# The output stage of a hybrid encoder layer in written order on every engine, with the sums of the first column group made in DRAM

## The chip, the core and the metric

The kernel runs on one core of a Trainium2 chip. Five engines work side by side: TensorE (PE, with its weight loads PEld), VectorE (DVE), ScalarE (ACT), GpSimd (POOL) and SyncE (SP, which only issues transfers). Each works through its own instructions in order; semaphores tie them together. Transfers run on 16 DMA engines and are issued from SP's queue or POOL's. The metric is the device time of one execution in microseconds (us).

## The reference

One layer over 512 tokens of width 2048, in float32. A combined projection `w_in` gives queries, keys, values, the attention's gate and the two inputs of a linear recurrent unit (LRU). Attention (8 heads) and the LRU (both directions) each give 1024 columns; each is normed as a group, and one output projection mixes both:

```python
h = rms_norm(x, norm_w)
proj = jnp.einsum('bsd,de->bse', h, w_in)
q, k, v, g_attn, xr, g_lru = jnp.split(proj, SPLITS, axis=-1)
attn_out = attention_group(q, k, v, q_norm_w, k_norm_w)
lru_out = lru_group(xr, conv_w, conv_b, lru_wa, lru_ba, lru_wx, lru_bx, lru_lambda)
mixed = jnp.concatenate([rms_norm(attn_out, attn_norm_w) * jax.nn.silu(g_attn),
                         rms_norm(lru_out, lru_norm_w) * jax.nn.silu(g_lru)], axis=-1)
return x + jnp.einsum('bse,ed->bsd', mixed, w_out)
```

The last line, `mixed` times `w_out` (512x2048 by 2048x2048) plus x, is the output stage.

## The kernel before

**Arithmetic.** A float32 operand is split into a rounded part `h` and a rest `l`; a product is three matmuls, hh + hl + lh. ScalarE makes `h` by a cast (`wh`), VectorE makes `l` by a subtraction (`wl`). A matmul is 128x128 by 128x512, written "mm" or "pj" after the PSUM bank it sums into.

**Stages.** The start transposes x, sums its squares and runs the first projection (0 to 57 us), with `rstd` per token on POOL (`rsqrt_mean`, L264 and L265), spread to the row `rbc` by `rows` (L275, L276, L278, a matmul L284 and a copy L285); then `evac_bc` (L383) multiplies projection results by `rbc`. The LRU's halves and the projections of keys, values and queries follow, woven with each other (to 279 us); the attention, woven with gate projections (279 to 446); the last two gate projections with the norms of both groups (446 to 507.5; the row scales of the attention's norm are `group_rstd`, L664 and L668, and `rows` again, `gbc`); and the output stage (507.6 to 682).

**The output stage.** 512x2048 by 2048x2048 is done in blocks of 2 by 2 by 2: seven products of blocks instead of eight. Its eight row pairs `i` (256 rows of `w_out` each) are gone through for two column groups `g` of 1024 columns. For each group a first half runs the pairs with products P1, Q6, Q5, Q7 (24 matmuls a pair), a second half with Q3, P2, Q4 (18 a pair). I number the pairs of halves 0 to 31: 0 to 7 and 8 to 15 are the halves of group 0, 16 to 23 and 24 to 31 those of group 1. Left sides (`mh`, `ml`) are built before, by `build`. The right sides are two blocks of `w_out` or sums of them: T1 and T3 are two-block sums (`t1`, `t30`, `t31`), T2 is x's first part plus a block, T4 is T2 plus another block. A right side for two products is a tile of 2 x 512 columns, `x_` or `y_`, which `split` (L720 cast, L721 subtraction) makes into `wh` and `wl`, in one of four buffers by turns, so a pair takes two of them.

Before the change, T1 and T3 are summed in DRAM: a copy on SP's queue and an accumulating transfer on POOL's (`sums_of_blocks`, L741 to L744, one row pair at each eighth fill step of the second projection; T1's accumulation in `other_sums`, L750, at the end of the query projection). T2 is `y_[:, 0] + x_[:, 0]` on VectorE (L790), is written to DRAM (`t2`, L792, POOL's queue) and read back in the second half (L833), where VectorE adds the other block (L836).

**What sets the order.** Except at the start, where more engines are written by hand, only TensorE's order is the written one. On the other engines a scheduler orders instructions, with the output stage's loads, splits and sums put early by a priority:

```python
SOON = 150
with tc.high_priority(SOON):
    nc.sync.dma_start(y_[:, 0], block(m, 1, 2 * g))
    nc.sync.dma_start(y_[:, 1], t3[g][m])
    xb = split(x_)
    nc.vector.tensor_add(y_[:, 0], y_[:, 0], x_[:, 0])
    yb = split(y_)
    nc.gpsimd.dma_start(t2[m], y_[:, 0])
```

Tiles loaded there come from two rings (`wring`, three tiles; `aring`, four) and a few kept buffers, so a load waits until the tile's former content has been split. In the attention POOL scales each weight tile (`weights`, L591), once per iteration; the tile is turned and used two iterations later.

Of the kernel before, what the change touches and what calls it, by code (L numbers as in the profile page):

```python
# [16 lines left out]
P = 128  # L17
# [41 lines left out]
def hybrid_kernel(  # L59
# [133 lines left out]
    loads_done, powers = {}, []  # L193
# [68 lines left out]
    def rsqrt_mean(dst, src, n, width):  # L262

        nc.gpsimd.tensor_scalar(dst, src, 1.0 / n, EPS, op0=ALU.mult, op1=ALU.add)  # L264
        powers[:] = [nc.gpsimd.tensor_tensor(dst, dst, nhalf[:, :width], op=ALU.pow).ins]  # L265
# [312 lines left out]

    def weights(q, g, t):
# [11 lines left out]
        nc.gpsimd.tensor_scalar(p, p, sm, 0.0, op0=ALU.mult, op1=ALU.add)  # L591
# [30 lines left out]
    def attention(rots):  # L622
# [4 lines left out]
        for i in range(last + 3):  # L627
            h, t = divmod(i, NT)
            if i < last:
                ps_[i] = weights(qs[h], h // G, t)  # L630
                if t == 0 and h + 2 < NH:
                    qs[h + 2] = turned(rots[(h + 2) // G], (h + 2) % G)
# [78 lines left out]
    def split(blocks):  # L711
# [7 lines left out]
        hi, lo = (t[:, : blocks.shape[1]] for t in (hi, lo))  # L719
        nc.scalar.copy(hi, blocks)  # L720
        nc.vector.tensor_sub(lo, blocks, f(hi))  # L721
# [5 lines left out]
    t1, t2, t30, t31 = (  # L727
        dram.tile([NP, P, SEQ + 16], F32, name=t, tag=t)[:, :, :SEQ] for t in ("t1", "t2", "t30", "t31")
# [7 lines left out]
    def sums_of_blocks():  # L736

        for m in range(NP):
            with tc.issue_after(loads_done[nc.sync]):
                for g in range(2):  # L740
                    nc.sync.dma_start(t3[g][m], block(m, 0, 2 * g))  # L741
                nc.sync.dma_start(t1[m], block(m, 0, 0))
            for g in range(2):
                nc.gpsimd.dma_start(t3[g][m], block(m, 1, 2 * g), accum_op=ALU.add)  # L744
            yield

    def other_sums():
        with tc.issue_after(*powers):
            for m in range(NP):
                nc.gpsimd.dma_start(t1[m], block(m, 0, 1), accum_op=ALU.add)  # L750

    def outputs(g, places, work):
# [3 lines left out]


        xs = [
            pools["out"].tile([P, NT, SEQ], F32, tag=t, bufs=1, name=nm(t)) for t in ("xt", "cb")
        ]  # L760

        def banks(*kinds):
            return [[kind() for _ in range(2)] for kind in kinds]

        def product(k, dst, i, b, n):
# [9 lines left out]
        p1, q6, q5, q7 = banks(*((mm, mm, pj, pj), (pj, mm, mm, pj))[g])  # L775
        for i in range(8):
            m = mixed[i][0] // (2 * P)
            with tc.high_priority(SOON):

                x_, y_ = next(places)(), next(places)()  # L780
                if g == 0:
                    nc.sync.dma_start(x_[:, 0], t1[m])
                    nc.sync.dma_start(x_[:, 1], block(m, 0, 1))
                else:
                    nc.sync.dma_start(x_.rearrange("p j e -> p (j e)"), block(m, 0, 2 * g, 2))
                    nc.vector.tensor_add(x_[:, 0], x_[:, 0], x_[:, 1])
                nc.sync.dma_start(y_[:, 0], block(m, 1, 2 * g))
                nc.sync.dma_start(y_[:, 1], t3[g][m])
                xb = split(x_)
                nc.vector.tensor_add(y_[:, 0], y_[:, 0], x_[:, 0])  # L790
                yb = split(y_)
                nc.gpsimd.dma_start(t2[m], y_[:, 0])  # L792
            next(work, None)
            for k, dst, b, n in ((P1, p1, xb, 1), (Q6, q6, yb, 0), (Q5, q5, xb, 0), (Q7, q7, yb, 1)):
                product(k, dst, i, b, n)
        with tc.high_priority(SOON):

            for s in range(2):
                nc.scalar.copy(xs[1][:, 2 + s], p1[s])
            for s in range(2):  # L800
                nc.vector.tensor_sub(xs[1][:, s], xs[1][:, 2 + s], q6[s])  # L801
            for s in range(2):
                nc.vector.tensor_sub(xs[0][:, 2 + s], q5[s], xs[1][:, s])  # L803
            for s in range(2):
                nc.vector.tensor_add(xs[0][:, s], q7[s], xs[0][:, 2 + s])  # L805
                nc.vector.tensor_sub(xs[1][:, s], xs[1][:, s], q7[s])  # L806

        def leave(t, j, queue, e0=0, e1=SEQ):
            c0 = (2 * g + j) * SEQ
            queue.dma_start(of[tokens[t], c0 + e0 : c0 + e1], xs[j][:, t, e0:e1])  # L810

        def residual(m, j):

            with tc.high_priority(SOON):
                xr = pools["fin"].tile([P, 2, SEQ], F32, tag="t4", bufs=2, name=nm("t4"))
# [5 lines left out]
            to = xs[j][:, 2 * m : 2 * m + 2]  # L821
            nc.vector.tensor_add(to, to, xr)  # L822

        q3, p2, q4 = banks(*((mm, mm, pj), (pj, mm, mm))[g])

        def second(i):
            m = mixed[i][0] // (2 * P)
            ring = (wring, aring)[i % 2]
# [15 lines left out]
        for i in range(8 - 2 * g):  # L844
            for step in second(i):
                step()
            if 1 <= i < 5:
                residual((i - 1) // 2, (i - 1) % 2)
# [267 lines left out]
```

## Time and profile before

| | |
|---|---|
| median of 3 runs (lowest, highest) | 689.21 us (688.12, 689.9) |
| the profiled execution, its time / its span | 688.86 us / 687.1 us |
| busy, share of the span: PE, DVE, ACT, POOL | 96%, 70%, 50%, 14% |
| mean granted TensorE clock | 0.981 |
| matmuls of the output stage (L771) | 672 |
| first L771 matmul, last L771 matmul | 507.58 us, 682.02 us |
| HBM read, written | 91.42 MB, 20.97 MB |

In a row of the timeline the columns are start, duration (us), engine, line, operation, out<-in, shapes, and in brackets the idle time before it with what ended it. "SPq" rows are transfers that SP issues. A DMA engine share is a mean over 16. In a row of groups, "busy, mean ns of one" and then the idle time before them with its releasers. A matmul's duration includes its drain, so start to start tells the pace.

### The profile page before, as it was taken

How to read it: one execution, taken by the hardware profiler on the slowest of the kernel's cores; microseconds unless marked ns; L12 is line 12 of the kernel's file. 1: busy time of each engine (PE TensorE's matmuls, PEld its weight loads, DVE VectorE, ACT ScalarE, POOL GpSimd, SP SyncE). 2: the span in 40 equal slices, each digit the busy share in tenths (PEclk: the TensorE clock that was granted, in tenths of full speed). 3: DMA queues.
4: the chain of work that ended last, by engine and by line, in shares of the span. 5: the costliest groups of instructions: out<-in, count | busy, mean ns of one | idle time of the engine just before them, and what ended most of it. 6: DMA issues, size and time to landing. Idle time of an engine off the chain costs nothing. (4 is left out here: it accounts for less than half of the span.)

```text
span 687.1 us, 8648 instructions
## 1 busy us (share of the span) xinstructions
PE 660.7 (96%) x3059; PEld 543.8 (79%) x3059; DVE 482.7 (70%) x788; ACT 340.2 (50%) x590; POOL 97.1 (14%) x137
## 2 busy tenths in 40 slices
PE   9998999999999999999999999979989989889997
PEld 6886888888888888888888888858868867668775
DVE  5868789968688747557655675788268677766774
ACT  3523798589668316445543474534245433234430
POOL 0011100100033105311222221000001102210010
PEclk9999999999999999999999999989989999999999
DMA  8867786842233323921122122214375848896562
GB/s 278 276 179 206 174 205 174 232 98 89 92 125 122 92 62 69 207 62 59 34 62 62 62 62 62 62 61 124 92 236 180 303 138 268 262 288 216 176 199 93
DMA packets 54140, 100.38 MB, mean 146 GB/s; under 512 B 4568, under 2 KB 14928, under 8 KB 54096
## 3 DMA queue, kind: packets, MB, share of 16 engines
q1 hardware_dynamic: 47088, 81.99, 37.8%
q0 software_dynamic: 6688, 17.31, 10.8%
q10 hardware_dynamic: 320, 0.53, 0.3%
q8 instruction: 24, 0.39, 0.2%
q14 instruction: 20, 0.16, 0.1%
HBM read 91.42 MB, written 20.97 MB: 164 GB/s over the span
## 5 line engine op out<-in xcount | busy, mean ns | idle before, releaser
L148 PE MATMUL pj<-x,wh 128*128 128x512 f32 x376 | 150.4, 400 | 2.8 <-DVE ev L383 2.8
L150 PE MATMUL pj<-x,wl 128*128 128x512 f32 x376 | 147.9, 393 | 0.0
L149 PE MATMUL pj<-x,wh 128*128 128x512 f32 x376 | 147.5, 392 | 0.0
L212 ACT CAST wh<-wr 128x512 fp32r<-128x512 f32 x143 | 85.9, 618 | 72.4 <-PE pj L150 25.9
L213 DVE TENSOR_TENSOR wl<-wr,wh 128x512 fp32r<-128x512 f32 x144 | 101.1, 725 | 29.0 <-ACT wh L212 24.9
L720 ACT CAST wh<-wr 128x1024 fp32r<-128x1024 f32 x64 | 60.0, 944 | 99.3 <-PE mm L771 61.3
L148 PEld LDWEIGHTS pj<-x,wh 128*128 128x128 f32 x376 | 71.4, 190 | 16.8 <-issue 3.2
L150 PEld LDWEIGHTS pj<-x,wl 128*128 128x128 f32 x376 | 71.1, 189 | 15.5
L149 PEld LDWEIGHTS pj<-x,wh 128*128 128x128 f32 x376 | 71.4, 190 | 14.0 <-DVE x L241 0.3
L148 PE MATMUL pj<-wh,x 128*128 128x512 f32 x192 | 74.9, 390 | 0.0
L150 PE MATMUL pj<-wh,x 128*128 128x512 f32 x192 | 74.7, 389 | 0.0
L149 PE MATMUL pj<-wl,x 128*128 128x512 f32 x192 | 74.7, 389 | 0.0
L721 DVE TENSOR_TENSOR wl<-wr,wh 128x1024 fp32r<-128x1024 f32 x64 | 67.2, 1085 | 9.3 <-ACT wh L720 9.1
L771 PE MATMUL mm<-wl,mh 128*128 128x512 f32 x128 | 51.9, 406 | 5.9 <-DVE wl L721 5.8
L771 PE MATMUL mm<-wh,mh 128*128 128x512 f32 x128 | 51.2, 400 | 1.9 <-ACT wh L720 1.9
L771 PE MATMUL mm<-wh,ml 128*128 128x512 f32 x128 | 51.2, 400 | 0.0
L600 ACT CAST b<-mm 128x512 fp32r<-128x512 f32 x32 | 18.8, 586 | 62.2 <-PE mm L598 62.2
L586 DVE TENSOR_REDUCE mx<-mm 128x1 f32<-128x512 f32 x32 | 22.1, 690 | 33.2 <-PE mm L150 32.4
L771 PE MATMUL pj<-wl,mh 128*128 128x512 f32 x96 | 39.0, 407 | 4.8 <-DVE wl L721 4.8
L150 PEld LDWEIGHTS pj<-wh,x 128*128 128x128 f32 x192 | 36.0, 188 | 7.6
L148 PEld LDWEIGHTS pj<-wh,x 128*128 128x128 f32 x192 | 36.0, 188 | 7.4
L149 PEld LDWEIGHTS pj<-wl,x 128*128 128x128 f32 x192 | 36.0, 188 | 7.4
(207 smaller groups left out, 1123.7 us busy)
## 6 DMA issues: line engine op xcount, KB each, us to landing
wr<-in_w_in_dram SPq DMA_DIRECT2D x71, 512.0 KB, 3.6
wr<-in_w_out_dram SPq DMA_DIRECT2D x24, 512.0 KB, 5.3
wr<-t SPq DMA_DIRECT2D x40, 256.0 KB, 5.1
t<-in_w_out_dram SPq DMA_DIRECT2D x24, 256.0 KB, 5.2
t<-in_w_out_dram POOLq DMA_DIRECT2D x24, 256.0 KB, 6.2
wr<-in_w_out_dram SPq DMA_DIRECT2D x24, 256.0 KB, 4.4
t<-wr POOLq DMA_DIRECT2D x16, 256.0 KB, 4.1
t<-in_x_dram POOLq DMA_DIRECT2D x8, 512.0 KB, 6.1
```

The source lines that it names most:

```text
L148: nc.tensor.matmul(acc, lh, rh, start=start, stop=False)
L149: nc.tensor.matmul(acc, lh, rl, start=False, stop=False)
L150: nc.tensor.matmul(acc, ll, rh, start=False, stop=stop)
L212: copy(hi, raw[:, k, :])
L213: nc.vector.tensor_sub(lo, raw[:, k, :], f(hi))
L586: nc.vector.tensor_reduce(mx, sc, axis=AX.X, op=ALU.max, negate=True)
L600: nc.scalar.copy(pth[:, :, tt], p3)
L720: nc.scalar.copy(hi, blocks)
L721: nc.vector.tensor_sub(lo, blocks, f(hi))
L771: nc.tensor.matmul(dst[s], lh[:, ts_], rh, start=i == 0 and j == 0, stop=i == 7 and j == 2)
```

## The change

It has four parts.

1. The output stage of all engines (ACT, DVE, SP, POOL beside PE) is in written order. Each pair's loads and splits are one generator, `feed1` or `feed2`, whose steps are called two pairs ahead (`feed(u + 2)`, one step between products and one after them). The first halves' products run P1, Q5, Q6, Q7, but for the last pair of a half, where P1, Q6, Q5, Q7 stays with the sums of the results between. The builds 5, 6, 7 and the last gates move into the stage's beginning.
2. For group 0, T1 to T4 are all made in DRAM. `first_sums` copies and adds T3 (both groups) and copies T1 and T2 (T2 from T3 of group 0); it starts at fill step 16 of the second projection and goes on in the query projection. `last_sums` adds to T2, copies T2 to T4, and adds to T1 and T4, one step after each weight tile of the attention. In group 1 T2 is kept on chip (`kept_t2`).
3. `group_rstd` and `rows` of the attention's norm get priority, and `rows` comes one fill step (six matmuls) later on TensorE. POOL's DRAM adds no longer stand ahead of `rstd`.
4. Group 1's output writes go on SP's queue (group 0's on POOL's), also the first two of them; its residual tiles of x come in the ring `aring`.

The number of 256 KB transfers from DRAM to DRAM goes from 48 to 80: 8 copies each to `t2` and `t4`, and 8 adds to each. In the output stage 16 stores of T2 and eight 256 KB loads of `w_out` go. VectorE has eight instructions fewer; TensorE has as many as before.

```diff
-    def sums_of_blocks():
-        for m in range(NP):
-            with tc.issue_after(loads_done[nc.sync]):
-                for g in range(2):
-                    nc.sync.dma_start(t3[g][m], block(m, 0, 2 * g))
-                nc.sync.dma_start(t1[m], block(m, 0, 0))
-            for g in range(2):
-                nc.gpsimd.dma_start(t3[g][m], block(m, 1, 2 * g), accum_op=ALU.add)
...
+    def first_sums():
+        for m in range(NP + 1):
+            if m < NP:
+                copy_to(*((t3[g][m], block(m, 0, 2 * g)) for g in range(2)))
+            if m:
+                for g in range(2):
+                    add_to(t3[g][m - 1], block(m - 1, 1, 2 * g))
+            yield
         for m in range(NP):
+            copy_to((t1[m], block(m, 0, 0)), (t2[m], t30[m]))
             yield
+    def last_sums():
+        for m in range(NP):
+            with tc.issue_after(last_scale[0]):
+                add_to(t2[m], block(m, 0, 1))
+            yield
+        for m in range(NP):
+            copy_to((t4[m], t2[m]))
+            yield
...
+    def feed1(g, i, got):
...
+        got.append(split(x_))
+        yield
+        y_ = next(places[g])()
+        nc.sync.dma_start(y_[:, 0], t2[m] if g == 0 else block(m, 1, 2 * g))
+        nc.sync.dma_start(y_[:, 1], t3[g][m])
+        if g == 0:
+            got.append(split(y_))
+        else:
+            z = kept_t2[i] = keep(i)
+            nc.vector.tensor_add(z, y_[:, 0:1], x_[:, 0:1])
+            got.append(split(z, y_[:, 1:2]))
+        yield
+    def feed2(g, i, got):
+        x_ = in_wr()
+        nc.sync.dma_start(x_.rearrange("p j e -> p (j e)"), block(m, 1, 2 * g, 2))
+        if g == 0:
+            z = in_av(1)
+            nc.sync.dma_start(z[:, 0], t4[m])
+        else:
+            z = kept_t2.pop(i)
+            nc.vector.tensor_add(z, z, x_[:, 1:2])
...
+                xb, yb = parts[u]
+                product(p1, i, P1, xb, 1)
+                if i < NP - 1:
+                    product(q5, i, Q5, xb, 0)
+                    next(work, None)
+                    feed(u + 2)
+                    product(q6, i, Q6, yb, 0)
+                    product(q7, i, Q7, yb, 1)
+                    feed(u + 2)
+                    continue
...
+                yield
+                to = xs[j][:, 2 * m : 2 * m + 2]
+                nc.vector.tensor_add(to, to, xr)
+                if (m, j) == (0, 0):
+                    for t in range(2):
+                        leave(t, 0)
...
-    fill = with_sums(fill, 8)
+    fill = with_sums(fill, 8, 16)
...
-    r = group_rstd(sums["a"], "r_a", NH * HD)
-    for _ in range(3):
+    with tc.high_priority():
+        r = group_rstd(sums["a"], "r_a", NH * HD)
+    for _ in range(4):
         next(fill)
-    rows(gbc, r, lambda: fin_s((P, NT, P), F32R))
+    with tc.high_priority():
+        rows(gbc, r, lambda: fin_s((P, NT, P), F32R))
```

How it moves instructions, at three places. First POOL's queue at the end of the first projection, before (`t_105`, `t_106` are `t30`, `t31`):

```order
12 L744 DMA t_105<-in_w_out_dram 128x512
13 L744 DMA t_106<-in_w_out_dram 128x512
14 L264 TENSOR_SCALAR rstd<-xsum 128x4
15 L265 TENSOR_TENSOR rstd<-rstd,nhalf 128x4
16 L744 DMA t_105<-in_w_out_dram 128x512
```

and now:

```order
12 L264 TENSOR_SCALAR rstd<-xsum 128x4
13 L265 TENSOR_TENSOR rstd<-rstd,nhalf 128x4
14 L750 DMA t_106<-in_w_out_dram 128x512
15 L750 DMA t_107<-in_w_out_dram 128x512
16 L750 DMA t_106<-in_w_out_dram 128x512
```

The two adds ahead of `rstd` now come behind it. Second, VectorE's queue around the sums of the attention's norm (`r_a`, then `part` and the two `s` of `rows`; `t` and `ml` belong to builds, `wl` to the last projections' weights), before:

```order
511 L696 TENSOR_TENSOR ml_4278<-t_885_4279,mh_4277 128x1024
512 L213 TENSOR_TENSOR wl_4443<-wr_4440,wh_4442 128x512
513 L213 TENSOR_TENSOR wl_4447<-wr_4440,wh_4446 128x512
514 L693 TENSOR_TENSOR t_888_4289<-hs_1704,t_888_4289 128x256
515 L668 COPY r_a<-mm_4353 128x4
516 L275 CAST part_4380<-r_a 128x4
517 L276 TENSOR_TENSOR part_4381<-r_a,part_4380 128x4
518 L278 TENSOR_TENSOR s_4382<-ident,part_4380 128x512
519 L696 TENSOR_TENSOR ml_4288<-t_888_4289,mh_4287 128x1024
520 L278 TENSOR_TENSOR s_4383<-ident,part_4381 128x512
```

and now:

```order
502 L213 TENSOR_TENSOR wl_4416<-wr_4413,wh_4415 128x512
503 L213 TENSOR_TENSOR wl_4420<-wr_4413,wh_4419 128x512
504 L694 TENSOR_TENSOR t_885_4312<-hs_1434 128x512
505 L671 COPY r_a<-mm_4386 128x4
506 L695 TENSOR_TENSOR t_885_4312<-hs_1434,t_885_4312 128x256
507 L275 CAST part_4429<-r_a 128x4
508 L699 TENSOR_TENSOR ml_4311<-hs_1434,mh_4310 128x768
509 L276 TENSOR_TENSOR part_4430<-r_a,part_4429 128x4
510 L278 TENSOR_TENSOR s_4431<-ident,part_4429 128x512
511 L278 TENSOR_TENSOR s_4432<-ident,part_4430 128x512
```

The copy stands earlier in the build of the row pair before (`t_885` instead of `t_888`), and both `s` follow each other. Third, SP's queue in group 1's second half (pairs 24 to 31), now; each `wr` of 128x1024 is the load of one pair, `xt` the first results to leave:

```order
216 L840 DMA wr_5744<-in_w_out_dram 128x1024
217 L840 DMA wr_5791<-in_w_out_dram 128x1024
218 L840 DMA wr_5834<-in_w_out_dram 128x1024
219 L840 DMA wr_5863<-in_w_out_dram 128x1024
220 L896 DMA out_dram<-xt_5471 128x512 x2
221 L840 DMA wr_5897<-in_w_out_dram 128x1024
222 L840 DMA wr_5929<-in_w_out_dram 128x1024
223 L840 DMA wr_5959<-in_w_out_dram 128x1024
224 L840 DMA wr_5989<-in_w_out_dram 128x1024
225 L896 DMA out_dram<-xt_5471 128x512 x2
```

Before, this stretch of SP's queue held two loads a pair, the block and T2 from DRAM, and no write before the last; the first two writes were on POOL's. And last VectorE's queue in the first half of group 1, now: one pair (L822 and L832 are the two sums, L726 the split's subtractions):

```order
631 L822 TENSOR_TENSOR wr_5453<-wr_5453 128x512
632 L726 TENSOR_TENSOR wl_5457<-wr_5453,wh_5456 128x1024
633 L832 TENSOR_TENSOR wr_5463<-wr_5460,wr_5453 128x512
634 L726 TENSOR_TENSOR wl_5466<-wr_5463,wh_5465 128x512
635 L726 TENSOR_TENSOR wl_5466<-wr_5460,wh_5465 128x512
636 L822 TENSOR_TENSOR wr_5493<-wr_5493 128x512
```

Before, a pair had two sums and two subtractions of 128x1024 there; now the second subtraction is in two parts, since T2 lies in a tile of its own.

More of the change, by code (lines that the diff above doesn't have):

```diff
@@ L752, in outputs, with copy_to, add_to @@
[L752 to L765, printed above, removed]
+    def copy_to(*pairs):
+        with tc.issue_after(loads_done[nc.sync]):
+            for dst, src in pairs:
+                nc.sync.dma_start(dst, src)
+    def add_to(dst, src):
+        nc.gpsimd.dma_start(dst, src, accum_op=ALU.add)
@@ L808, in leave, with banks @@
[L808 to L815, printed above, removed]
+        def banks(*kinds):
+            return [[kind() for _ in range(2)] for kind in kinds]
+        with tc.high_priority(SOON):
+            for u in (0, 0, 1):
+                feed(u)
@@ new lines, in residual @@
+                to = xs[j][:, 2 * m : 2 * m + 2]
[3 more added lines that the diff above has]
+                        leave(t, 0)
+                yield
+            rs = [residual(n // 2, n % 2) for n in range(4)]
+            next(rs[0]), next(rs[1])
+            q3, p2, q4 = banks(*((mm, mm, pj), (pj, mm, mm))[g])
+            takes = ((q3, Q3, 0, 0), (p2, P2, 0, 1), (q4, Q4, 1, 0))
+            ends = ((2, 0), (2, 1), (0, 1))
```

251 lines of the change are left out of this document (147 added, 104 removed).

## The prediction

> **What bounds the kernel now.** I read the page's shares first, then TensorE's waits, then its timeline at each wait, then what the named engine did. From the page, the busy time and TensorE's row of 40 slices (17.2 us each):
>
> ```profile
> PE 660.7 (96%) x3059; PEld 543.8 (79%) x3059; DVE 482.7 (70%) x788; ACT 340.2 (50%) x590; POOL 97.1 (14%) x137
> PE   9998999999999999999999999979989989889997
> ```
>
> TensorE is busy 96% of the span, so only its gaps, and the slow clock behind them, can be won; its matmul count is unchanged. The row dips in the fourth slice, in the 27th (from 446.6 us), and five times from the 30th on. By stretch (length, busy time of PE, PEld, DVE, ACT, POOL, granted clock, DMA share, GB/s):
>
> ```profile
> 279.00:446.00 167.00, 167.00 (x901) 141.94 (x900) 105.65 (x184) 84.86 (x167) 33.34 (x42) 1.00 0.24 70
> 460.00:507.50 47.50, 47.50 (x211) 39.31 (x210) 25.62 (x38) 14.05 (x22) 1.15 (x2) 1.00 0.42 130
> 600.00:615.00 15.00, 12.39 (x48) 9.74 (x47) 8.86 (x12) 6.00 (x6) 2.71 (x5) 0.89 0.92 296
> ```
>
> The attention (first row) and the last projection (second) lose nothing; a piece of the output stage (third) does. TensorE's waits (total, times, longest):
>
> ```profile
> PE mm L771 <- DVE wl L721: 5.8, 5, 2.1
> PE mm L284 <- DVE s L278: 5.0, 2, 4.1
> PE pj L771 <- DVE wl L721: 4.8, 3, 2.6
> PE pj L148 <- DVE ev L383: 2.8, 1, 2.8
> PE mm L771 <- ACT wh L720: 1.9, 1, 1.9
> ```
>
> Three places: the column scales `rbc` (L383 at 57.7 us), the row scales of the attention's norm (L284 at 450.6), and the right sides of the output (L720/L721). A wait costs more than itself. TensorE's timeline at one of them, and the output stage's first and last matmul:
>
> ```profile
> 507.58 0.39 PE L771 MATMUL mm<-wh,mh 128*128 128x512 f32 x1
> ...
> 602.20 0.39 PE L771 MATMUL pj<-wh,mh 128*128 128x512 f32 x1
> ...
> 603.56 0.39 PE L771 MATMUL pj<-wh,mh 128*128 128x512 f32 x1
> 606.55 0.68 PE L771 MATMUL pj<-wl,mh 128*128 128x512 f32 x1 [2.61 <-DVE wl L721]
> 607.02 0.63 PE L771 MATMUL pj<-wh,ml 128*128 128x512 f32 x1
> 607.45 0.63 PE L771 MATMUL pj<-wh,mh 128*128 128x512 f32 x1
> ...
> 682.02 0.39 PE L771 MATMUL mm<-wh,ml 128*128 128x512 f32 x1
> ```
>
> At full pace a matmul starts every 1.36 us / 6 = 0.227 us (602.20 to 603.56). After the wait the pitch is 0.43 for some seven matmuls. So the stage's 672 matmuls need 152.3 us, and took 682.02 + 0.23 − 507.58 = 174.7: **22.4 us lost** in the output stage.
>
> **Early place 1, `rbc`.** POOL, ScalarE, VectorE and TensorE there:
>
> ```profile
> 43.86 1.92 POOL L744 DMA_DIRECT2D t<-in_w_out_dram  x2 [42.22 <-DMA t<-in_w_out_dram]
> 46.13 1.04 POOL L265 TENSOR_TENSOR rstd<-rstd,nhalf 128x4 f32<-128x4 f32 x1
> 47.21 0.17 DVE L275 CAST part<-rstd 128x4 fp32r<-128x4 f32 x1 [4.76 <-POOL rstd L265]
> 53.23 0.62 ACT L408 CAST k<-k 128x512 fp32r<-128x512 f32 x1 [2.53 <-DMA k<-in_lru_wx_dram]
> 53.88 0.69 DVE L409 TENSOR_TENSOR k<-k,k 128x512 fp32r<-128x512 f32 x1 [2.48 <-ACT k L408]
> 60.95 0.77 PE L148 MATMUL pj<-x,wh 128*128 128x512 f32 x1 [2.85 <-DVE ev L383]
> ```
>
> The rstd stands behind two DRAM adds that POOL could only issue at 43.86; the change takes them from ahead of it. VectorE had idled since 42.4, so rstd, now two short operations, lets it resume at about 45 instead of 47.2: 2.1 us. The 2.48 us that VectorE waits at L409 is also open: in the new order five more small operations (some 0.2 us apart) precede it, 1.0 us of cover, and the copies no longer ahead on SP may let the load land sooner. The loss is the wait of 2.85, a slow first matmul (0.77 instead of 0.39), and some seven at 0.43 after it, 0.2 each: 4.7. Gain between 1.0 (the load lands as before) and 4.7; nearer the upper since both causes shrink: **3.2**.
>
> **Early place 2, row scales.** VectorE and TensorE:
>
> ```profile
> 445.79 0.95 PE L664 MATMUL mm<-ones,asum 128*128 128x1 f32 x8
> 452.43 0.15 DVE L668 COPY r_a<-mm 128x4 f32<-128x4 f32 x1
> 454.30 0.68 DVE L278 TENSOR_TENSOR s<-ident,part 128x512 fp32r<-128x512 f32 x1
> 455.04 0.79 PE L284 MATMUL mm<-s,ones_r 128*128 128x512 f32 x1 [4.08 <-DVE s L278]
> 456.78 0.80 PE L284 MATMUL mm<-s,ones_r 128*128 128x512 f32 x1 [0.94 <-DVE s L278]
> ```
>
> The sums were in PSUM at 446.7, but the copy to r_a stood behind weight splits until 452.43. In the new order two splits and one 512-wide operation stand ahead of it and then it comes, so `s` is ready near 451. TensorE stood at 455.04 − 4.08 = 451.0 and now wants it six matmuls later, 452.3. Waits of 4.08 and 0.94, two slow first matmuls (0.4 each) and some six at 0.43 (0.2 each) made 7.0; start to start over pace it is 7.3. Gain **7.2**: what VectorE puts off is hidden in the last projection, where it is busy 25.6 of 47.5 us. If `s` came 1 us after TensorE, 6.
>
> **Output stage, part by part.** Means of the forms, in the stretch from 520 us on:
>
> ```profile
> L721 DVE TENSOR_TENSOR wl<-wr,wh 128x1024 fp32r<-128x1024 f32 x43 | 51.8, 1219 | 3.2 <-ACT wh L720 3.1
> L720 ACT CAST wh<-wr 128x1024 fp32r<-128x1024 f32 x43 | 45.0, 1053 | 87.2 <-PE mm L771 59.4 <-PE pj L771 16.5 <-DVE wr L786 8.9
> L836 DVE TENSOR_TENSOR wr<-wr,wr 128x512 f32<-128x512 f32 x16 | 11.0, 690 | 18.8 <-DMA wr<-t 18.8
> L721 DVE TENSOR_TENSOR wl<-wr,wh 128x512 fp32r<-128x512 f32 x16 | 10.9, 684 | 0.0
> L720 ACT CAST wh<-wr 128x512 fp32r<-128x512 f32 x16 | 9.9, 622 | 5.3 <-PE pj L771 3.5 <-PE mm L771 1.8
> ```
>
> Today L836 waits 18.8 us for T2 to come back from DRAM, ahead of the splits on VectorE. In group 0 the change takes out eight L790 and eight L836 adds (16 x 0.69 = 11 us of VectorE) and the round trip; in group 1 the round trip only. Every split has two pairs (8 to 11 us) of lead. What is left, from the written order and these durations:
>
> - Pair 0: y0's cast cannot start before the last projection ends, since its buffer is free only then; cast 1.05, two splits of 1.2 and four evacuations put Q6's banks free about 3.9 us in, when TensorE gets there at 2.7. **1.2** (0 to 3).
> - Pair 17: its left part's feed stands behind group 0's six end sums of 0.69. **0.4** (0 to 1.3).
> - Group 1, first half: VectorE's chain per pair is add 0.69, cast 1.05, split 1.22, add 0.69, cast 0.62, splits 0.68 + 0.68 = 5.6, against 24 x 0.227 = 5.44 for TensorE. Six pairs at 0.1: **0.6** (to 2).
> - Pairs 23 and 24: Q6 comes second in the last pair, so y's split is wanted earlier, and the next pair waits for its banks: **1.25 + 0.85**.
> - Pair 28: on SP's queue two writes of `xt` now wait for a residual sum and stand ahead of this pair's load:
>
> ```profile
> 677.04 1.02 SPq L810 DMA_DIRECT2D out_dram<-xt  x2
> ...
> wr<-in_w_out_dram SPq DMA_DIRECT2D x24, 512.0 KB, 5.3
> ...
> wr<-in_w_out_dram SPq DMA_DIRECT2D x4, 512.0 KB, 3.9
> ```
>
>   (issuing takes 0.5 us a write; such a load lands in 5.3 over the whole run, in 3.9 from 640 us on, the last row). From the start of pair 26: two products 2.7 and the writes' issue make 3.6; landed 7.5 to 8.9; cast and split 9.8 to 11.2; wanted after two pairs of 18 x 0.227, at 8.2. **1.6 to 3.0, taken 1.8** by the nearer row. Pair 31, whose load waits for a split just ahead: **0.7**.
>
> Sum left over: 1.2 + 0.4 + 0.6 + 1.25 + 0.85 + 1.8 + 0.7 = 6.8 (3 to 13 with the ends). Gain 22.4 − 6.8 = **15.6**.
>
> Should a left wait bring the slow clock, it costs about 2 more. In the trace 2.61 did, as shown, and so did 1.87 (the matmul behind it took 0.67, not 0.39):
>
> ```profile
> 510.97 0.67 PE L771 MATMUL mm<-wh,mh 128*128 128x512 f32 x1 [1.87 <-ACT wh L720]
> ```
>
> I charge none in the sum, for my longest single wait is 1.8, and put 2 to 4 into the upper end. The Trainium skill ("TensorE: Matmul & The Clock Gate", section "Part 1: The HAM clock gate") says that the clock falls to half after an idle window of about 3.4 us, and by that rule nothing I leave would cost a slow clock: the sum stays. The trace does not agree, since waits of 1.87 and 2.61 us were enough, and by the trace the sum could rise by those 2 to 4.
>
> **Attention.** It takes on 24 DRAM adds on POOL's queue and 8 copies on SP's.
>
> ```profile
> 283.50 0.82 POOL L750 DMA_DIRECT2D t<-in_w_out_dram  x1 [1.77 <-issue]
> 289.60 0.69 POOL L591 TENSOR_SCALAR k<-k,sm 128x512 f32<-128x512 f32 x1 [2.62 <-DVE sm L590]
> 294.01 0.69 POOL L591 TENSOR_SCALAR k<-k,sm 128x512 f32<-128x512 f32 x1 [3.72 <-DVE sm L590]
> ```
>
> An issue of 0.82 behind a scale of 0.69 fits into the 2.6 to 3.7 us that POOL waits before the next. DMA engines are busy 0.24 there, so the 8 MB added cost nothing. A weight tile is turned two iterations, 8 us or more, after its scale: without that cover each add would cost its 0.82, 20 us in all. Hence 0.
>
> **Sum.** 7.2 + 3.2 + 15.6 = 26.0 from the profiled execution's 688.86 (its span is 687.1, and the 1.8 around it stays) gives 662.9. That execution is 0.35 under the median of 689.21, so I forecast **663**.
>
> **Rivals.**
> 1. The strict order costs more. VectorE's semaphore hops raise group 1's chain from 5.6 to 6.1 per pair (7 x 0.66 = 4.6 instead of 0.6), pair 0 waits its 3, and two waits bring the slow clock: 4.0 + 1.8 + 4 = 9.8 more, **673**. For it: ScalarE and VectorE alternate in that chain and 5.6 already exceeds 5.44. Against: the lead of two pairs absorbs the first microseconds.
> 2. All waits vanish: 22.4 + 7.3 + 4.7 = 34.4 off, **655**. For it: DMAs can be issued far ahead. Against: pair 28's SP queue and pair 0's buffer, which no lead mends.
> 3. Slower: loads land too late for VectorE, which in written order holds everything behind the late split. The DMA share is 0.92 at 600 to 615 us now, and loads lead by about two pairs, 8 to 11 us. If they landed in 12 us, over twice the 5.3, each of 32 pairs would wait 1 us or more, and one in four the slow clock too (2 us): 32 + 16 = 48, against the 26 gained: +22, **711**. It decides from 26 / 32 = 0.8 us a pair on. Against: bytes in the output stage fall, as 16 stores of T2 go.
> 4. The change does not do what it says early: both early places keep their wait, since something else on VectorE takes the place. Then only 15.6: **673.5**, by another way.
>
> **Chances.** Forecast 0.62 (its own range 657 to 671), rival 1 0.16, rival 2 0.10, rival 3 0.04, rival 4 0.06, which leaves 0.02 near no change. The range **655.5 to 676** holds all but rival 3, the remnant and most of rival 2. A change under 0.3% (2 us) cannot be told from none. Faster 0.94, within 0.3% 0.02, slower 0.04.
>
> **What would show it.** Right: no TensorE wait at L284 and at most 2 us at L383; the slices from 27 on at 9; the waits on the splits' VectorE row down from 12.5 us to about 7, at the first pair, between the 17th and 24th, and at the 28th; the same 4.9 us or so from the last matmul to the end (687.1 − 682.2). Wrong: waits of TensorE for POOL's scales in the attention, a wait at every pair of the output, or a granted clock under 0.95 throughout it.

## The result, and the profile after

The changed kernel takes 666.62 us (median of 4 runs, 665.31 to 668.48) against 689.56 us before (4 runs, 688.12 to 690.12): a ratio of 0.967 with a 95% interval of 0.964 to 0.970, 22.9 us less. Forecast were 663 us and 655.5 to 676. The profiled execution took 665.31 us with a span of 663.5, so the traces account for 688.86 − 665.31 = 23.55 us.

From the page of the changed kernel, its busy time, TensorE's row of slices (now 16.6 us each) and the granted clock:

```profile
PE 651.9 (98%) x3059; PEld 539.0 (81%) x3059; DVE 473.7 (71%) x780; ACT 340.7 (51%) x598; POOL 99.7 (15%) x135
PE   9999999999999999999999999999999999999977
PEclk9999999999999999999999999999999999999989
```

The dips in the fourth and 27th slices are gone, and those of the output stage up to the 38th. What remains stands in the last two. By stretch (columns as before):

```profile
57.00:65.00 8.00, 8.00 (x37) 6.64 (x36) 7.82 (x13) 4.24 (x7) 0.00 (x0) 1.00 0.41 130
275.00:440.00 165.00, 165.00 (x891) 140.31 (x890) 104.05 (x181) 84.36 (x167) 50.34 (x63) 1.00 0.53 112
440.00:460.00 20.00, 20.00 (x93) 16.66 (x92) 18.42 (x31) 8.39 (x12) 1.32 (x2) 1.00 0.28 79
636.00:648.00 12.00, 8.19 (x29) 6.02 (x28) 8.92 (x11) 4.80 (x6) 0.00 (x0) 0.86 0.45 159
```

Both early places (57 to 65, 440 to 460) lose nothing. The attention takes its 24 adds (POOL busy 50 instead of 33 us, DMA share 0.53 instead of 0.24) and loses nothing either. One stretch of 12 us in the output stage holds the largest loss. TensorE's waits:

```profile
PE pj L873 <- ACT wh L725: 3.1, 1, 3.1
PE pj L873 <- DVE wl L726: 1.4, 2, 0.8
PE pj L873 <- DVE ev L383: 1.3, 1, 1.3
PE mm L873 <- DVE wl L726: 0.2, 1, 0.2
```

and its timeline where they lie, with the stage's first and last matmul:

```profile
495.61 0.39 PE L873 MATMUL mm<-wh,mh 128*128 128x512 f32 x1
...
499.77 0.47 PE L873 MATMUL pj<-wh,mh 128*128 128x512 f32 x1 [1.28 <-DVE ev L383]
...
579.81 0.50 PE L873 MATMUL pj<-wl,mh 128*128 128x512 f32 x1 [0.65 <-DVE wl L726]
...
616.26 0.50 PE L873 MATMUL mm<-wl,mh 128*128 128x512 f32 x1 [0.23 <-DVE wl L726]
...
639.79 0.50 PE L873 MATMUL pj<-wh,mh 128*128 128x512 f32 x1 [3.06 <-ACT wh L725]
641.05 0.51 PE L873 MATMUL pj<-wl,mh 128*128 128x512 f32 x1 [0.76 <-DVE wl L726]
...
641.78 0.63 PE L873 MATMUL pj<-wh,mh 128*128 128x512 f32 x1
...
658.65 0.39 PE L873 MATMUL mm<-wh,ml 128*128 128x512 f32 x1
```

Counting matmuls from the stage's start places them: 12 before the first wait (Q6 of pair 0), 361 before the second (pair 17), 511 before the third (Q6 of pair 23), 600 before the fourth (pair 28). The stage began 12.0 us earlier than before (495.61 instead of 507.58), which is 4.6 from `rbc` and 7.3 from the row scales. It took 658.65 + 0.23 − 495.61 = 163.3 us, 11.0 over its 152.3, where it had lost 22.4: 11.4 won. 12.0 + 11.4 = 23.4 of the 23.55.

The 11.0 left are, in start to start over pace: pair 0 1.43, pair 17 0.82, pair 23 0.50, pair 28 3.21 + 1.03, the slow clock behind pair 28 (0.63 long matmuls, until 645) 1.7, and 2.3 in gaps under 0.3. Of these small gaps, which are too short for the list of waits, 1.5 us lie at pairs 18 to 23, a quarter of a us in each: the second matmul of each of these pairs starts as the first split of the pair ends. VectorE there, where the same operations come back every 5.73 us, against the 24 x 0.227 = 5.44 us of TensorE's matmuls:

```profile
584.26 1.23 DVE L726 TENSOR_TENSOR wl<-wr,wh 128x1024 fp32r<-128x1024 f32 x1 [1.25 <-ACT wh L725]
585.40 0.68 DVE L832 TENSOR_TENSOR wr<-wr,wr 128x512 f32<-128x512 f32 x1
586.85 1.29 DVE L726 TENSOR_TENSOR wl<-wr,wh 128x512 fp32r<-128x512 f32 x2 [0.76 <-ACT wh L725]
...
589.99 1.22 DVE L726 TENSOR_TENSOR wl<-wr,wh 128x1024 fp32r<-128x1024 f32 x1 [1.25 <-ACT wh L725]
```

VectorE waits for ScalarE's casts (1.25 + 0.76 us a pair) and ScalarE for VectorE's sums, so neither is full and the two together set the pace of group 1's first half.

### The profile page after: what moved, and what is told of

Read it like the earlier page. It is cut to its first block, busy times and chain, and to the rows that moved or that the text cites. A ratio compares the mean times of both kernels' runs of the same rounds, so it can differ in the third digit from the quotient of the medians.

```text
span 663.5 us, 8655 instructions
## 1 busy us (share of the span) xinstructions
PE 651.9 (98%) x3059; PEld 539.0 (81%) x3059; DVE 473.7 (71%) x780; ACT 340.7 (51%) x598; POOL 99.7 (15%) x135
## 4 chain that ended last, share of the span: by engine, by line
PE 86%; DVE 6%; DMA 3%; ACT 2%; issue 1%; SPq 0%; ACTq 0%; DVEq 0%; POOL 0%; POOLq 0%
PE pj L148 19%; PE pj L150 19%; PE pj L149 19%; PE mm L873 8%; PE pj L873 5%; DVE wl L726 3%; PE mm L148 3%; PE mm L150 3%; PE mm L149 3%; DMA wr<-t 3%; PE mm L600 2%; ACT wh L725 2%; PE mm L238 1%; PE pj L304 1%; DMA wr<-in_w_out_dram 1%
## 5 line engine op out<-in xcount | busy, mean ns | idle before, releaser
L725 ACT CAST wh<-wr 128x1024 fp32r<-128x1024 f32 (+1 forms) x72 | 60.0, 859 | 85.9 <-PE mm L873 19.0
L726 DVE TENSOR_TENSOR wl<-wr,wh 128x1024 fp32r<-128x1024 f32 (+1 forms) x72 | 68.4, 982 | 35.4 <-ACT wh L725 35.4
L149 PEld LDWEIGHTS pj<-x,wh 128*128 128x128 f32 x376 | 70.7, 188 | 13.8 <-DVE x L241 0.3
L148 PEld LDWEIGHTS pj<-x,wh 128*128 128x128 f32 x376 | 70.6, 188 | 13.2
L873 PE MATMUL mm<-wl,mh 128*128 128x512 f32 x128 | 50.3, 393 | 0.2 <-DVE wl L726 0.2
L750 POOL DMA_DIRECT2D t<-in_w_out_dram x40 | 33.1, 841 | 101.9 <-DMA t<-in_w_out_dram 101.5
L150 PEld LDWEIGHTS pj<-wh,x 128*128 128x128 f32 x192 | 36.0, 188 | 7.6
L873 PE MATMUL pj<-wh,mh 128*128 128x512 f32 x96 | 37.8, 394 | 4.3 <-ACT wh L725 3.1
```

The source lines that it names most:

```text
L148: nc.tensor.matmul(acc, lh, rh, start=start, stop=False)
L149: nc.tensor.matmul(acc, lh, rl, start=False, stop=False)
L150: nc.tensor.matmul(acc, ll, rh, start=False, stop=stop)
L725: nc.scalar.copy(hi[:, to], b)
L726: nc.vector.tensor_sub(lo[:, to], b, f(hi[:, to]))
L750: nc.gpsimd.dma_start(dst, src, accum_op=ALU.add)
```

## The experiments

The runs of the kernel before that stand beside these experiments have a median of 687 to 688 us, from 682.0 to 691.5; the changed kernel is taken at 666.62, from a comparison in which the kernel before had 689.56. A difference from 666.62 is therefore uncertain by some 2 to 3 us, and differences of that size are read from the traces.

### The writes behind the loads

In pair 28 the load was issued only behind two writes. SP, VectorE and ScalarE of the changed kernel:

```profile
630.87 1.21 DVE L947 TENSOR_TENSOR xt<-xt,wr 128x1024 f32<-128x1024 f32 x1
632.11 0.82 SPq L896 DMA_DIRECT2D out_dram<-xt  x2
633.04 8.31 SPq L840 DMA_DIRECT2D wr<-in_w_out_dram  x4
638.69 2.51 ACT L725 CAST wh<-wr 128x1024 fp32r<-128x1024 f32 x3 [8.75 <-DMA wr<-in_w_out_dram]
```

The sum ends at 632.1, the writes go, the load follows at 633.04 and lands 5.6 us later. The edit:

```diff
-                if (m, j) == (0, 0):
-                    for t in range(2):
-                        leave(t, 0)
...
                 feed(u + 2)
+                if i == LATE[g]:        # LATE = (2, 5)
+                    for t in range(2):
+                        leave(t, 0)
```

> The changed kernel with one edit: the first two output writes of a group's second half no longer stand directly behind their residual sum, but behind the loads (in group 1 behind the load of pair 31, on SP's queue). Theory (pair 28's load waits on SP's queue behind writes that wait for a sum): in the changed kernel's profile TensorE lost 3.21 + 1.03 us there, and the matmuls behind it ran at a slow clock until about 647, some 3.5 us more; all of it goes, 7 to 8 us less than the changed kernel's 666.6, about 659. Rival (the load is late because its place in the ring comes free late, or because loads from DRAM take 5.6 us there): the wait stays at 2 us or more and the time within 2 us of 666.6. If the wait goes but the slow clock comes at another place, 4 us less.

Measured: 659.21 us (658.77 to 659.32), 7.4 less than the changed kernel (6.0 from profiled execution to profiled execution, 665.31 to 659.32, which is the 3.21 + 1.03 + 1.7 of above; the profiled one was the fastest of the changed kernel's four). Waits of TensorE in that run's output stage:

```profile
PE pj L875 <- DVE ev L383: 1.3, 1, 1.3
PE pj L875 <- DVE wl L726: 0.7, 1, 0.7
PE mm L875 <- DVE wl L726: 0.2, 1, 0.2
```

The wait of 3.1 on ScalarE is gone with the slow clock behind it, and nothing has come in its place. The rival falls: pair 28's load is issued at 623.24 instead of 633.04, so its ring had room. Slow landing had a part in the wait, though: in the changed kernel three loads went out behind the two writes within 1.0 us, and two of them landed in 5.6 and 7.1 us; here the two loads that follow pair 28's, issued 2.3 us apart, landed in 3.5 and 3.8. Whether the bunching made the difference was not tried.

### The evacuations first

```diff
-            for u in (0, 0, 1):
-                feed(u)
-        next(work)
-        feed(1)
+            feed(0)
+            next(work)          # evacuations of acc[:2]
+            feed(0)
+            next(work)          # evacuations of acc[2:]
+            feed(1)
+        feed(1)
         next(work)
```

> The changed kernel with one edit: at the output stage's start the four evacuations of the last gate projection stand earlier on VectorE, two ahead of y0's split and two ahead of x1's. Theory (pair 0's wait of 1.28 us is VectorE's order: two splits of 1.2 us ahead of the evacuations that free Q6's banks): the wait goes, 1.3 to 1.5 us less than the changed kernel. Rival (y0's cast, which can start only as the last projection ends, sets it): the wait moves from L383 to the split of y0 and stays at about 1 us, no change beyond 0.5 us.

Measured: 664.73 us (663.79 to 665.57), 1.9 less than the changed kernel, which is no more than the uncertainty. The trace decides: the output stage has no wait ahead of pair 17, and the profiled execution takes 663.79 instead of 665.31. Pair 0's wait was the order on VectorE, as the theory says, and its 1.4 us go with it.

### Two early parts alone, in the kernel before

The part on the attention's norm:

```diff
-    r = group_rstd(sums["a"], "r_a", NH * HD)
-    for _ in range(3):
+    with tc.high_priority():
+        r = group_rstd(sums["a"], "r_a", NH * HD)
+    for _ in range(4):
         next(fill)
-    rows(gbc, r, lambda: fin_s((P, NT, P), F32R))
+    with tc.high_priority():
+        rows(gbc, r, lambda: fin_s((P, NT, P), F32R))
```

> The kernel before with only the part on the attention's norm (priority of its group sums and row scales, and the rows six matmuls later). Theory: the two waits of TensorE at L284 (4.08 and 0.94 us) and the slow clock behind them go, 7.2 us less than before, about 682. Rival (VectorE's postponed builds come due and are late elsewhere before the output stage): 3 us or less.

Measured: 678.47 us (675.57 to 680.99), a ratio to before of 0.989 (0.983 to 0.995): 8.5 less, the interval 3 to 12. The trace has the size: TensorE has no wait at L284, and between 448 and 463 us it wins 7.3 us on the profile before. The theory's 7.2 holds. In this one execution the wait at 57 us, which the edit does not touch, was longer (3.4 us), so the output stage begins only 5.8 us earlier.

The DRAM sums later, which puts `rstd` ahead of them on POOL:

```diff
-    fill = with_sums(fill, 8)
+    fill = with_sums(fill, 8, 16)
...
+    drain(wsums)
     other_sums()
```

> The kernel before with only the start of its DRAM sums moved from the first to the seventeenth fill step of the second projection (and what is left of them issued ahead of T1's sums), so that no DRAM add stands ahead of rstd on POOL. Theory: the wait of 2.85 us for L383 at 57.7 us and the slow clock behind it go, 4.7 us less than before, about 685. Rival (the load of lru_wx, which landed at 53.2, holds VectorE at L409 as before): 1 us less. Nothing else should change by more than 1 us.

Measured: 686.76 us against 686.98, ratio 0.9999 (0.996 to 1.003): nothing. The wait at 57 us is gone as the theory says. But the sums left over were put by the scheduler ahead of the norm of the LRU's group (`r_l`), the same fault at another place. POOL, VectorE and the stretch in that run (columns as above):

```profile
235.45 0.82 POOL L744 DMA_DIRECT2D t<-in_w_out_dram  x1 [4.18 <-issue]
236.34 0.19 POOL L264 TENSOR_SCALAR r_l<-r_l 128x4 f32<-128x4 f32 x1
237.68 0.17 DVE L275 CAST part<-r_l 128x4 fp32r<-128x4 f32 x1 [6.59 <-POOL r_l L265]
...
230.00:242.00 12.00, 9.22 (x44) 7.17 (x44) 4.45 (x10) 1.83 (x3) 2.86 (x4) 1.00 0.83 186
```

TensorE lost 2.8 us there, and more behind it: the output stage begins at 506.64, 0.9 us earlier than before. So the sums were packed closer, to be through in time:

```diff
-    fill = with_sums(fill, 8)
+    fill = with_sums(fill, 5, 16)
```

> The kernel before with only the start of its DRAM sums moved to the seventeenth fill step of the second projection, at every fifth step so that all eight row pairs are through before the queries' norm. Theory (in the run with the later sums, the wait for L383 at 57 us went, and its 4.7 us were given back at 236 us since a DRAM add stood ahead of r_l's two operations on POOL): no wait at L383 and none at 236 us, 4.7 us less than before in the profile's early part. Rival (the time is lost elsewhere before 279 us in any case, for instance through transfers that now fall together with the weights' loads): the stretch up to the attention is as long as in the kernel before.

Measured: 687.52 us against 687.7: nothing again. No wait at 57 or at 236 us, but one of 2.7 us at 96. The stretch, and ScalarE:

```profile
80.00:100.00 20.00, 17.32 (x76) 14.01 (x76) 13.78 (x24) 15.69 (x23) 4.11 (x5) 1.00 1.05 253
97.72 0.62 ACT L408 CAST k<-k 128x512 fp32r<-128x512 f32 x1 [4.23 <-DMA k<-in_lru_wx_dram]
98.25 3.00 ACT L435 ACTIVATE b<-mm,vec 128x512 f32<-128x512 f32 x5
```

The DMA engines are full (a share of 1.05) and a small load of `lru_wx` lands late; the activations that TensorE waits for stand behind its cast. In the kernel before the share of the same stretch was 0.81. Against the next run, where this does not happen, that load was issued 1.8 us later (92.36 instead of 90.54) and took 5.3 instead of 2.4 us to land. The rival of this run, that transfers now fall together, is what happened; the output stage begins at 506.49, 1.1 us earlier than before. Last, the changed kernel's own pace, eight steps apart and going on in the queries' projection:

```diff
-    fill = with_sums(fill, 8)
+    fill = with_sums(fill, 8, 16)
...
-    fill = both()
+    fill = with_sums(both(), 5)
...
+    drain(wsums)
     other_sums()
```

> The kernel before with the start of its DRAM sums at the seventeenth fill step of the second projection, at every eighth step as there, and going on in the keys' and then the queries' projection at the changed kernel's pace, so that no add is left ahead of r_l and transfers are not bunched. Theory (two earlier tries lost the 4.7 us again by their own faults: an add ahead of r_l at 236 us, and transfers bunched at 80 to 100 us, with a DMA share of 1.05, that made a load late): no wait of TensorE between 57 us and the attention, the output stage begins 4.7 us earlier than in the profile of the kernel before, at 502.9, and the time falls by 3 to 5. Rival (the gain of 4.7 us is always taken back by the chain of the LRU behind it, and stands in the changed kernel for another reason): the output stage begins at 506 to 507.6 and the time is the same.

Measured: 682.75 us (12 runs) against 687.55 (17 runs), a ratio of 0.993 (0.991 to 0.995): 4.8 less. The stretches from 57 us to the attention:

```profile
57.00:80.00 23.00, 23.00 (x103) 19.05 (x102) 17.93 (x27) 16.36 (x27) 2.42 (x3) 1.00 0.64 172
80.00:100.00 20.00, 20.00 (x90) 16.57 (x89) 16.81 (x28) 19.34 (x29) 2.82 (x4) 1.00 0.82 198
100.00:279.00 179.00, 179.00 (x805) 148.35 (x804) 137.74 (x207) 113.12 (x233) 35.52 (x44) 1.00 0.52 135
```

TensorE loses nothing in 222 us. It wins 4.5 us at 57 us and keeps them to the attention. The output stage begins at 504.71, 2.9 earlier instead of 4.7: in this one execution the start, where TensorE now waited 1.2 + 0.3 us at two places of the first projection (L304), had cost 0.7, and 1.0 more went at the row scales, where this kernel still has the waits of the kernel before and a longer slow clock came behind them. So the early part is won in full only with the sums paced so that they are neither ahead of a norm nor bunched.

### The order, the lead, and T2 in DRAM

Three edits of the changed kernel each take back one idea. The written order:

```diff
-    last.enter_context(tc.manual_schedule(engines={E.Activation, E.DVE, E.SP, E.Pool}))
...
-                next(feeds[u])
+                with tc.high_priority(SOON):
+                    next(feeds[u])
```

> The changed kernel with the written order taken from ScalarE, VectorE, SP and POOL in the output stage (the scheduler orders them, the feeds with the kernel before's priority); sums in DRAM, lead of two pairs and products' order stay. Theory (the order is what removes the output stage's waits): the scheduler puts x0's split behind the four evacuations, four gate products and a build on VectorE (some 2.4 + 2.6 + 4 us after the last projection), so pair 0 waits 6 to 9 us with a slow clock, and splits of later pairs wait behind sums of pairs ahead: 8 to 14 us more than the changed kernel, 675 to 681. Rival (T2's way through DRAM was the cause, the order does little): within 3 us of 666.6.

Measured: 677.75 us (675.43 to 678.89), 11.1 more. VectorE at the stage's start in that run:

```profile
496.93 0.95 DVE L699 TENSOR_TENSOR ml<-av,mh 128x768 fp32r<-128x768 f32 x1
497.80 1.22 DVE L699 TENSOR_TENSOR ml<-t,mh 128x1024 fp32r<-128x1024 f32 x1
...
501.81 4.62 DVE L726 TENSOR_TENSOR wl<-wr,wh 128x1024 fp32r<-128x1024 f32 x4
```

A build's operations run ahead of the first four splits, though TensorE waits for these; it loses 8.5 us at pair 0. It loses 2.9 more at pair 12 and 6.5 at pair 16, whose banks come free late because group 0's end sums stand behind sums and splits of later pairs. The total lies in the theory's 8 to 14 us, and pair 0 is as it says. At pair 16 the order is the reverse of what it names: sums stand behind splits there, not splits behind sums.

The lead of two pairs:

```diff
-                    feed(u + 2)
+                    feed(u + 1)
```

(at every place, with the start and the end fitted to it)

> The changed kernel with each feed one pair ahead instead of two, everything else in the same written order. Theory (the lead covers cast and split): first halves have 2.72 us from a feed to its use, against 1.05 + 1.22 in group 0 and 0.69 + 1.05 + 1.22 = 2.96 in group 1; second halves 1.36 us against 2.27 to 2.96, so 0.7 to 1.4 us in each of 14 pairs, and 5 to 9 at the three changes of halves and the end: 15 to 25 us more, 682 to 692. Rival (loads far ahead are enough, the splits are quick): under 5 us more.

Measured: 673.66 us (672.13 to 675.79), 7.0 more. Both expectations miss: more than the rival's 5, less than half of the theory's 15 to 25. The waits:

```profile
PE pj L873 <- ACT wh L725: 4.8, 2, 2.6
PE pj L873 <- DVE wl L726: 2.8, 4, 0.9
PE mm L873 <- DVE wl L726: 2.3, 5, 0.8
PE mm L873 <- ACT wh L725: 1.6, 1, 1.6
```

By the count of matmuls they lie at pairs 1, 2, 8, 13, 16, 23 to 25 and 27; the two of 2 us and more are pair 16, behind the six end sums, and pair 27. Most pairs of the second halves wait for nothing, so the expectation's 0.7 to 1.4 us in each of 14 pairs was wrong. The traces show why: a written lead is a place in the queue and not a time. In the middle of group 0's second half ScalarE casts as soon as TensorE has left a buffer, so pair 12's first split ends 3.16 us ahead of its use with one pair of lead (556.69, 559.85) as with two (554.07, 557.23). The lead counts where VectorE's queue is held by something else: by gates and a build at the first pairs, by end sums at the changes of halves, and for 4.96 us by a residual tile of x ahead of pair 13's split. At pair 27 VectorE waits 5.20 us for that pair's own load, which again stands behind the two writes.

T2 of group 0 on chip, alone and with the late writes:

```diff
-        nc.sync.dma_start(y_[:, 0], t2[m] if g == 0 else block(m, 1, 2 * g))
+        nc.sync.dma_start(y_[:, 0], block(m, 1, 2 * g))
...
         if g == 0:
+            nc.vector.tensor_add(y_[:, 0], y_[:, 0], x_[:, 0])
             got.append(split(y_))
```

> The changed kernel with group 0's T2 summed on VectorE (0.69 us a pair more there, y loaded from the weights instead of T2 from DRAM); T4 still comes from DRAM, and T2 is still made there for it. Theory (with written order and two pairs of lead VectorE has room): in pairs 0 to 6 VectorE's splits, gates, builds and these sums make about 36 us in 38, so 0 to 2 us more than the changed kernel. Rival (group 0's T2 in DRAM is what the gain needs, VectorE becomes the bound of the first half): 4 us more or above, with waits of TensorE on splits from pair 2 on.

> The run with group 0's T2 on chip, with the late writes beside it, so that pair 28's wait is out of the comparison; to be set against the late writes alone (659.2). Theory (group 0's first half is then bound by VectorE and ScalarE in turn, cast behind sum and split behind cast, with gates and builds between): the seven waits of pairs 2 to 6 stay, some 6 us, 664 to 667. Rival (in the run with T2 on chip the loss came mostly of pair 28's longer wait): 661 or less.

Measured: 674.78 us (674.31 to 676.23), 8.2 more than the changed kernel; with the late writes 667.78 (666.64 to 669.12), 8.6 more than the late writes alone. The theory of the first run (0 to 2 us, since VectorE has 36 us of work in 38) falls and its rival holds; pair 28 is not the cause. In the second run, the seven waits at pairs 2, 3, 5 and 6 come to 6.0 of the 8.6 us, as expected; the time is 0.8 over the expected range. ScalarE and VectorE there:

```profile
518.61 2.36 DVE L726 TENSOR_TENSOR wl<-wr,wh 128x1024 fp32r<-128x1024 f32 x2 [1.16 <-ACT wh L725]
520.89 0.69 DVE L829 TENSOR_TENSOR wr<-wr,wr 128x512 f32<-128x512 f32 x1
521.74 1.05 ACT L725 CAST wh<-wr 128x1024 fp32r<-128x1024 f32 x1 [2.21 <-DVE wr L829]
522.82 1.23 DVE L726 TENSOR_TENSOR wl<-wr,wh 128x1024 fp32r<-128x1024 f32 x1 [1.25 <-ACT wh L725]
...
525.49 0.95 DVE L699 TENSOR_TENSOR ml<-av,mh 128x768 fp32r<-128x768 f32 x1
```

The sum (L829) stands between two splits, so the next cast must wait for it, and the next split for the cast (1.25 us idle): per pair not 0.69 but up to the sum and a cast that nothing covers, 0.69 + 1.05. With the operations of a build in the same pair (the last line is one) the lead is used up. T2 in DRAM takes the sum out of this chain.

### The group change, and a faster version

Three edits together: late writes, evacuations first, and pair 17's left part fed ahead of the last two end sums of group 0.

> The changed kernel with the late writes (659.2 alone), the earlier evacuations (1.4 us of waiting gone in its profile), and pair 17's first feed ahead of the last two of group 0's six end sums. Theory: three separate waits, so the gains add: 659.2 - 1.4 - 0.8 = 657.0, with a single wait of about 0.2 us left at pair 24. Rival (VectorE is short of time at the group change, so that the q4 sums come late and Q7 of pair 16 waits for their banks): 0.8 us or more more, 658 to 659.

Measured: 657.72 us (657.39 to 657.77), 0.7 more than the theory. The wait of pair 17 is gone, and Q7 of pair 16 waits instead:

```profile
577.37 0.47 PE L875 MATMUL pj<-wh,mh 128*128 128x512 f32 x1 [1.75 <-DVE cb L908]
575.40 1.23 DVE L726 TENSOR_TENSOR wl<-wr,wh 128x1024 fp32r<-128x1024 f32 x1 [1.25 <-ACT wh L725]
576.54 1.28 DVE L908 TENSOR_TENSOR cb<-cb,pj 128x512 f32<-128x512 f32 x2
```

VectorE idles 1.25 us for the cast and then splits, while the sums that free Q7's banks stand behind: the rival of this run. So the feed was cut in two, with sums of p2 in the cast's time:

```diff
             nc.vector.tensor_add(x_[:, 0], x_[:, 0], x_[:, 1])
+            if i == 1:
+                yield
...
                         last(t0, j, dst)
+                        if k != Q4:
+                            feed(u + 2)
```

> The changed kernel with the late writes and the earlier evacuations as in the run with three edits, but pair 17's first feed cut in two: its sum stands behind the first two end sums of group 0, its split behind the next two, so that VectorE sums p2 while ScalarE casts. Theory (the wait for the q4 sums in the run with three edits came of VectorE standing idle during that cast, 1.1 us): both the wait of pair 16 (1.91 us lost there) and that of pair 17 (0.82) go, 657.7 - 1.9 = 655.8. Rival (the work at the group change is simply too much for VectorE): a wait of 0.5 us or more remains at pair 16 or 17, 656.5 to 658.

Measured: **656.70 us** (656.54 to 656.80), a ratio to before of 0.9545 (0.952 to 0.957), the fastest of all. Its waits in the output stage:

```profile
PE pj L877 <- DVE cb L910: 0.5, 1, 0.5
PE mm L877 <- DVE wl L726: 0.2, 1, 0.2
```

0.9 more than the theory's 655.8: of the 1.91 lost at pair 16, 0.70 remain, as the rival has it.

## Why the prediction was right, and where not

- **The sum.** 26.0 us were forecast off the profiled execution and 23.55 came. The time fell near the forecast with some luck: the early places gave 1.5 more than taken, which hides a third of the 4.2 by which the output stage fell short.
- **What bounds the kernel.** Right: TensorE's gaps were all there was to win; 23.4 of 23.55 us are gaps and slow clock that went. Four of the places named (pairs 0, 17, 23 and 28) are those where TensorE still waits.
- **`rbc`, taken 3.2.** 4.6, near the upper end of 4.7. Both causes went: `part` ran at 43.44 instead of 47.21, and the load of `lru_wx` was there by 49.48 instead of 53.23:

```profile
43.44 0.17 DVE L275 CAST part<-rstd 128x4 fp32r<-128x4 f32 x1 [1.22 <-POOL rstd L265]
49.48 0.62 ACT L408 CAST k<-k 128x512 fp32r<-128x512 f32 x1 [1.20 <-DMA k<-in_lru_wx_dram]
```

  What the prediction did not see is that this gain hangs on the pace of the sums for the next 180 us. In two of the three runs that try it in the kernel before, all but about 1 us of it was given back.
- **Row scales, taken 7.2.** 7.3; `s` ready before TensorE came, as worked out.
- **Output stage, 15.6.** 11.4, the term that was mis-sized. By place, taken and measured: pair 0 1.2 and 1.43; pair 17 0.4 and 0.82; group 1's first half 0.6 and 1.5; pair 23 1.25 and 0.50; pair 24 0.85 and nothing; pair 28 1.8 and 4.24; pair 31 0.7 and nothing. Seven terms with sum 6.8 came to 8.5, with errors both ways; the rest of the 11.0 is the slow clock, next point, and 0.8 in gaps that had no term. The largest miss is pair 28. Its mechanism was right to the row of the queue, and two durations in it were short: the load was issued 4.6 us after pair 26's start (628.4, two pairs of 18 matmuls ahead of 636.6) and not 3.6, since the sum of 1.2 us had been left out, and it landed in 5.6 us, near the 5.3 of the whole run, not in the 3.9 of the rows from 640 us on, which were taken as "nearer". This is the step that failed. In group 1's first half the mechanism was right too, and the size short twice: the forecast's own 5.6 against 5.44 makes 0.16 a pair and not 0.1, and the chain took 5.73.
- **The slow clock, charged at none.** It cost 1.7 of the 11.0. The prediction had 2 to 4 in the upper end, with the rule that the Trainium skill gives ("TensorE: Matmul & The Clock Gate", section "Part 1: The HAM clock gate") beside rows that spoke against it. The wait of 3.06 us with one of 0.76 behind it brought it, at a granted clock of 0.86 from 636 to 648 us. Each is shorter than the window of about 3.4 us that the Trainium skill names; the measurement decides against the rule here as it did before.
- **T2's change, no price of its own.** The prediction counted the 11 us of VectorE that it saves and gave the gain to the list of waits as a whole. The runs put a price on the parts: without group 0's T2 in DRAM +8.2, without the written order +11.1, with one pair of lead +7.0. Their sum is far over the 11.4 that the output stage gained, so the parts depend on each other; how was not tried.
- **Attention, nothing.** Right.
- **Rivals.** Landings of 12 us, the slower case, did not come. Of the strict order's costs (rival 1) one slow clock came, and its main term in part: VectorE's chain in group 1's first half took 5.73 us a pair instead of its 6.1 and cost 1.5 us instead of 4.6. The 666.62 lies between the forecast's 663 and this rival's 673.

## What to carry to other kernels

An engine's queue in written order moves the waits to where one can read them; then look in each queue for an instruction that waits for a result, and at what stands behind it: two output writes of 0.4 us each cost some 6 us here by the traces, because a load stood behind them. A lead written into a queue is a place and not a time: here it counted only where something between held the queue. A sum that lies between cast and split of the same chain costs more than its length, since the other engine waits for it and is waited for. Pace background transfers: the same 16 sums cost nothing, or most of a gain of 4.7 us, by whether they stood ahead of a small operation or filled the DMA engines in one stretch.

## What the runs showed that was not expected

- **The times became narrow.** Over four runs each, the kernel before beside it and the changed kernel spread by 2.0 and 3.2 us, the version with late writes by 0.55 (658.77 to 659.32) and the fastest by 0.3. (Over all comparisons, 54 runs, the kernel before ran between 682.0 and 691.5.) That the spread comes from waits which hang on a transfer's landing fits this, but was only argued.
- **The slow clock has no sharp edge in the length of one wait.** Waits of 1.75 us (pair 16 in the run with three edits), 2.01 (at 593.71 in the profile before) and 2.72 (at 569.78 in the run with the scheduler's order) left the pitch at 0.23; 1.87 (at 510.97 before, with a second of 0.67 behind it), 2.08 (at 564.54 before, five matmuls later) and 2.61 (at 606.55 before) brought 0.43. What decides between them stays open.
